# Padded token tiles and eight unread one-column matmuls in a decoder layer on one Trainium2 core

## The chip, the cores and the metric

The kernel runs on one core of one Trainium2 chip. The metric is the device time of one execution in microseconds (us), as a median over several runs. A core has a matmul engine (TensorE, PE in the profile; PEld is its weight load), a vector engine (VectorE, DVE), a scalar engine (ScalarE, ACT), GpSimd (POOL) and SyncE (SP), which issues most DMAs. They run side by side and wait for each other by semaphores. A matmul takes a stationary operand of 128 x 128 (the weights) and streams a moving operand of N columns past it; its result goes to one of eight banks of PSUM, each 512 fp32 columns wide.

## The reference

One step of a hybrid decoder layer is computed for 1024 prompt tokens and 64 sample tokens with shared weights. The part that matters here is the feed-forward block at its end:

```python
def conv_ffn(h, w_up, conv_w, conv_b, w_down, prev):
    z = h @ w_up
    T = z.shape[1]
    zp = jnp.concatenate([prev, z], axis=1)
    c = conv_b + sum(zp[:, j:j + T] * conv_w[j] for j in range(CONV_W))
    a, b = jnp.split(c, 2, axis=-1)
    return (jax.nn.gelu(a) * b) @ w_down, zp[:, T:]
...
    x = x + merged @ w_out
    f, nconv = conv_ffn(rmsnorm(x, norm_ffn), w_up, conv_w, conv_b, w_down, conv_prev)
    return x + f, nk, nv, nconv, vn
```

`w_up` has 1024 rows and 5632 columns, `w_down` 2816 rows and 1024 columns. Ahead of this block stand the input projection, windowed attention, a chunked gate and two output projections; a final RMSNorm stands behind it.

## The kernel before

All products are fp32 in three matmuls: each operand is split into a high and a low part (`th`, `tl` for tokens, `wh`, `wl` for weights), and high x high, low x high and high x low are added in one bank. The splits run on ScalarE (L40, a cast) and VectorE (L41, a subtraction).

The large projections go by a scheme of Strassen's kind: a 2 x 2 block product is made of seven half-size products. The class `Chain` does this for one group of tokens. Group 0 has two halves of 288 columns, group 1 two halves of 256. A token tile holds, for one of four blocks of 128 rows, the seven operands side by side, so `T0` tiles are 7 x 288 and `T1` tiles 7 x 256 columns of 4 bytes. `T0` lies at the right end of the on-chip memory, eight tiles one behind the other, made in `t0_split` (L1562): for each row block the high tile and then the low one. `product(j, w)` (L291) issues the j-th product: 12 matmuls on L301 (four row blocks, three of high and low each) into one bank, and then a copy or an addition that reads the bank.

The up projection (L1699 to L1777) runs over 22 column blocks f. The first three (`FEW`, L1700) run group 0 alone, 7 x 12 matmuls of 288 columns each. Then a loop over `order` (L1756, counter `at`) runs both groups on the 19 others, and group 1 alone on blocks 0, 1 and 2, which stand at `at` 6, 13 and 21. Which group goes first alternates from product to product (L1770), so that two products of 256 columns and two of 288 follow each other in turn: 24 matmuls of one width, 24 of the other. Between the blocks `finish` does convolution, gate and the token operands of the down projection, which go to memory.

The down projection (L1921 to L1958) has 77 units, eleven (`NU`) for each of seven products; `at` counts the products here, `lo` the unit within one. A unit loads and splits a token tile (a ring of tiles of 576 columns) and one half weight tile, and issues 24 matmuls on L1804: four column blocks of 288 columns and four of 256, three matmuls each. Near the end `fin_rms` (L1832) and `fin_rb` (L1848) put small fp32 matmuls of the final norm between units; each of these instructions stands in the trace as two matmuls, called passes below. They use a bank of their own (`psl`).

The order on each engine is that of the code, as the tile scheduler lays it out. Token tiles of the up projection are written once before it; weights come by a ring four deep.

Of the kernel before, what the change touches and what calls it, by code (L numbers as in the profile page):

```python
# [6 lines left out]
F32 = mybir.dt.float32  # L7
F32R = mybir.dt.float32r
# [7 lines left out]
P = 128  # L16
# [18 lines left out]
def layer(tc, a):  # L35
    nc = tc.nc
    V, S, G, PE = nc.vector, nc.scalar, nc.gpsimd, nc.tensor
# [9 lines left out]
    with ExitStack() as top:  # L47
# [26 lines left out]
        ones = cst.tile([P, P], F32, name="c_ones")  # L74
        V.memset(ones, 1.0)
        ident = cst.tile([P, P], F32, name="c_ident")
# [184 lines left out]
        def combine(t4, b11, b12, b21, b22):  # L261
# [3 lines left out]
            V.scalar_tensor_tensor(t4[:, 1], t4[:, 2], -1.0, b11, ALU.mult, ALU.subtract)  # L265
            V.scalar_tensor_tensor(t4[:, 3], t4[:, 1], -1.0, b21, ALU.mult, ALU.subtract)

        def wt(i):
            return a["wt"][i].rearrange("p (k c) -> p k c", c=P)

        class Chain:

# [15 lines left out]
                for to, lo, hi in self.places(e, half):  # L288
                    op(to, pick(x, to, lo, hi), pick(y, to, lo, hi))  # L289

            def product(self, j, w):  # L291
                name = "adadaca"[j]
                first = name not in self.bank
                if first:
                    self.bank[name] = self.ps.tile([P, 512], F32, name="st")[:, :self.n2]
                ps = self.bank[name]
                wh, wl = w
                for kk in range(4):
                    th, tl = (x[:, (0, 1, 2, 6, 3, 5, 4)[j]] for x in self.tx[kk])
                    for i, (u, v) in enumerate(((wh, th), (wh, tl), (wl, th))):  # L300
                        PE.matmul(ps, u[:, kk, :], v, start=first and kk + i == 0,  # L301
                                  stop=kk == 3 and i == 2, skip_group_check=True)
                kept = self.kept
                if j == 0:
                    self.keep("1", ps)
                elif j == 1:
                    self.keep("5", ps)
                elif j == 2:
                    self.keep("u", ps)
                elif j == 3:  # L310
                    self.put(0, 1, V.tensor_add, kept["u"], ps)
                elif j == 4:
                    self.keep("n", ps, -1.0)
                    self.put(1, 1, G.tensor_sub, kept["n"], kept["5"])
                elif j == 5:
                    self.put(0, 0, V.tensor_add, kept["1"], ps)
                else:
                    for to, lo, hi in self.places(1, 0):
                        S.activation(to, pick(ps, to, lo, hi), AF.Copy, scale=-1.0)
# [39 lines left out]
        with ExitStack() as ph1:  # L359
# [1198 lines left out]
            def t0_split(kk):  # L1558

                def go():  # L1560
                    x0, x1, t4 = hx.pop(kk)
                    tx[0][kk] = th, tl = tuple(t0p.tile([P, 7, 288], F32R, name=f"t{y}0{kk}") for y in "hl")  # L1562
                    split(th[:, 0], tl[:, 0], x0[:, 0:288])
                    split(th[:, 5:7], tl[:, 5:7], x1.rearrange("p (h c) -> p h c", h=2))
                    split(th[:, 1:5], tl[:, 1:5], t4)
                return go
# [189 lines left out]
        for at, f in enumerate(order):  # L1756
            if at == NFF - 1:
                t0o.close()
                dn_pools()
                zp.update(z=right(tops, "z2"), za=1)  # L1760
            za, zb = z_pair()
            if f < FEW:
                for e, z in enumerate((za, zb)):
                    nc.sync.dma_start(z[:, 0:594], zd[f][e])
            else:
                put_state(f, (za, zb))
            chains = [up_chain(g, za, zb) for g in ((1,) if f < FEW else (0, 1))]
            for j in range(7):
                w = W.get(3, 1)
                for ch in chains[::1 - 2 * ((7 * at + j) % 2)]:  # L1770
                    ch.product(j, w)
                if f < FEW and j == 3:
                    put_state(f, (za, zb))
            if at < NFF - 2:
                finish(f, za, zb)
            else:
                later.append(lambda f=f, za=za, zb=zb: finish(f, za, zb))  # L1777
        pse.close()

        with ExitStack() as ph3:  # L1780
# [115 lines left out]
            def units(n, count):  # L1896
                out = []
                for x in range(n, n + count):
                    t_upto(x + 5, x + 3)
                    w = W.get(2, 3)  # L1900
                    out.append((w, ts["made"][x]))
                return out
# [18 lines left out]
            for at, j in enumerate(DN_ORDER):  # L1921
# [4 lines left out]
                for lo, hi in blocks:  # L1926
# [10 lines left out]
                    for go in hooks.get((at, lo), ()):  # L1937
                        go()
                    got = units(n0 + lo, hi - lo)
                    for mp in range(2) if hi - lo == 2 else (0,):  # L1940
                        for e in range(2):
                            for x in range(lo, hi):
                                for m in range(2 * mp, 2 * mp + 2) if hi - lo == 2 else range(4):
                                    mm_dn(m, e, x, got[x - lo], new)
                        if hi == NU:
                            for m in (2 * mp, 2 * mp + 1):
                                for e in range(2):
                                    take(j, m, e)
# [134 lines left out]
```

## Time and profile before

| | us |
|---|---|
| median of three runs (lowest, highest) | 1504.83 (1504.61, 1505.7) |
| profiled execution, its own time | 1506.5 |
| its span, first to last instruction | 1504.6 |
| PE busy | 1492.3 |
| DVE, ACT, POOL busy | 1163.4, 832.7, 282.5 |
| L301, share of the chain that ended last | 52% |
| L1804, share of the chain that ended last | 15% |

The profile shows one execution on the hardware. Busy times are sums over an engine's instructions; matmuls overlap, so PE at 99% does not say how close it is to its peak. The clock row gives the granted clock of PE in tenths of full speed, slice by slice. The chain is followed back from the last instruction. In the timeline the first column is the start of an instruction and the second its duration; the difference of two starts is what passes from one matmul to the next.

### The profile page before, as it was taken

How to read it: one execution, taken by the hardware profiler on the slowest of the kernel's cores; microseconds unless marked ns; L12 is line 12 of the kernel's file. 1: busy time of each engine (PE TensorE's matmuls, PEld its weight loads, DVE VectorE, ACT ScalarE, POOL GpSimd, SP SyncE). 2: the span in 40 equal slices, each digit the busy share in tenths (PEclk: the TensorE clock that was granted, in tenths of full speed). 3: DMA queues.
4: the chain of work that ended last, by engine and by line, in shares of the span. 5: the costliest groups of instructions: out<-in, count | busy, mean ns of one | idle time of the engine just before them, and what ended most of it. 6: DMA issues, size and time to landing. Idle time of an engine off the chain costs nothing.

```text
span 1504.6 us, 31437 instructions
## 1 busy us (share of the span) xinstructions
PE 1492.3 (99%) x12169; PEld 1479.7 (98%) x12169; DVE 1163.4 (77%) x1954; ACT 832.7 (55%) x1798; POOL 282.5 (19%) x438
## 2 busy tenths in 40 slices
PE   9999999999999999999999999999999999999998
PEld 8999999999998999999999999999999999999998
DVE  6887779557545986988678888898898888785676
ACT  7656674554554775864444654654555556453463
POOL 2001003100030332430222222232142122000003
PEclk9999999999999999999999999999999999999999
DMA  8552468557659757859977423332332217973454
GB/s 282 182 189 104 165 216 270 176 177 249 216 209 326 236 177 237 246 190 315 337 242 271 142 102 121 119 123 95 116 131 95 109 64 243 362 235 98 121 185 134
DMA packets 136932, 286.10 MB, mean 190 GB/s; under 512 B 15312, under 2 KB 43856, under 8 KB 136784
## 3 DMA queue, kind: packets, MB, share of 16 engines
q1 hardware_dynamic: 131952, 279.57, 55.1%
q10 hardware_dynamic: 4832, 4.54, 0.9%
q8 instruction: 95, 1.56, 0.4%
q14 instruction: 53, 0.43, 0.1%
HBM read 195.56 MB, written 90.46 MB: 190 GB/s over the span
## 4 chain that ended last, share of the span: by engine, by line
PE 94%; DVE 3%; ACT 1%; issue 1%; DMA 0%; SPq 0%; DVEq 0%; ACTq 0%
PE st L301 52%; PE mm L241 15%; PE dn L1804 15%; PE st L538 6%; PE sc L1295 1%; PE po L1356 1%; PE mx L904 1%; PE pt L1328 1%; ACT s L1318 1%; DVE nm L1311 0%; DVE s L1321 0%; DVE s L1305 0%; DMA wh<-xt 0%; PE st L603 0%; DVE of L1367 0%
## 5 line engine op out<-in xcount | busy, mean ns | idle before, releaser
L301 PE MATMUL st<-th,wh 128*128 128x256 f32 (+1 forms) x2128 | 611.4, 287 | 0.3 <-ACT k L282 0.2
L301 PE MATMUL st<-tl,wh 128*128 128x256 f32 (+1 forms) x2128 | 609.7, 287 | 0.0
L301 PE MATMUL st<-th,wl 128*128 128x256 f32 (+1 forms) x2128 | 609.3, 286 | 0.0
L301 PEld LDWEIGHTS st<-th,wh 128*128 128x128 f32 x2128 | 400.6, 188 | 1.3 <-ACT k L282 0.9
L301 PEld LDWEIGHTS st<-th,wl 128*128 128x128 f32 x2128 | 400.9, 188 | 0.0
L301 PEld LDWEIGHTS st<-tl,wh 128*128 128x128 f32 x2128 | 400.4, 188 | 0.0
L40 ACT CAST wh<-wraw 128x512 fp32r<-128x512 f32 (+1 forms) x244 | 144.1, 611 | 85.3 <-PE st L301 33.6
L41 DVE TENSOR_TENSOR wl<-wraw,wh 128x512 fp32r<-128x512 f32 (+1 forms) x244 | 166.1, 696 | 27.3 <-ACT wh L40 25.4
L1804 PE MATMUL dn<-th,wh 128*128 128x288 f32 (+1 forms) x616 | 177.6, 288 | 0.0
L1804 PE MATMUL dn<-tl,wh 128*128 128x288 f32 (+1 forms) x616 | 177.1, 287 | 0.0
L1804 PE MATMUL dn<-th,wl 128*128 128x288 f32 (+1 forms) x616 | 177.0, 287 | 0.0
L40 ACT CAST wh<-ws 128x512 fp32r<-128x512 f32 x160 | 98.0, 622 | 96.5 <-PE st L301 78.3
L41 DVE TENSOR_TENSOR wl<-ws,wh 128x512 fp32r<-128x512 f32 x160 | 109.0, 694 | 50.4 <-ACT wh L40 48.7
L1804 PEld LDWEIGHTS dn<-th,wh 128*128 128x128 f32 x616 | 116.9, 190 | 0.0
L1804 PEld LDWEIGHTS dn<-th,wl 128*128 128x128 f32 x616 | 115.8, 188 | 0.0
L1804 PEld LDWEIGHTS dn<-tl,wh 128*128 128x128 f32 x616 | 115.8, 188 | 0.0
L289 POOL TENSOR_TENSOR z<-ku,k 128x256 f32<-128x256 f32 (+1 forms) x32 | 30.1, 943 | 317.2 <-ACT ku L284 242.4
L40 ACT CAST th<-traw 128x544 fp32r<-128x544 f32 (+1 forms) x85 | 54.1, 643 | 55.6 <-PE dn L1804 42.9
L41 DVE TENSOR_TENSOR tl<-traw,th 128x544 fp32r<-128x544 f32 (+1 forms) x85 | 61.0, 725 | 23.3 <-ACT th L40 23.1
L241 PE MATMUL mm<-s,wh 128*128 128x256 f32 (+1 forms) x384 | 76.5, 295 | 0.0
L282 ACT COPY k<-st 128x256 f32<-128x256 f32 (+1 forms) x152 | 56.0, 381 | 35.2 <-PE st L301 34.2
L241 PE MATMUL mm<-oh,wh 128*128 128x256 f32 (+1 forms) x256 | 73.6, 288 | 0.0
(311 smaller groups left out, 3187.2 us busy)
## 6 DMA issues: line engine op xcount, KB each, us to landing
wraw<-wt SPq DMA_DIRECT2D x133, 512.0 KB
traw<-td SPq DMA_DIRECT2D x77, 272.0 KB
td<-za SPq DMA_DIRECT2D x22, 544.0 KB
wraw<-wt SPq DMA_DIRECT2D x35, 256.0 KB
upd<-hl SPq DMA_DIRECT2D x14, 512.0 KB
td<-t SPq DMA_DIRECT2D x11, 544.0 KB
qd<-q SPq DMA_DIRECT2D x8, 576.0 KB
q<-qd SPq DMA_DIRECT2D x8, 576.0 KB
```

Of the source, the lines that this page charges most:

```text
L40: S.copy(hi, src)
L41: V.tensor_sub(lo, src, hi.bitcast(F32))
L241: PE.matmul(ps[:, lo:lo + c1 - c0], u[:, k, :], v[:, c0:c1], start=(clear and k == 0 and i == 0), stop=(k == nk - 1 and i == 2), skip_grou ...
L282: S.copy(t, src)
L289: op(to, pick(x, to, lo, hi), pick(y, to, lo, hi))
L301: PE.matmul(ps, u[:, kk, :], v, start=first and kk + i == 0, stop=kk == 3 and i == 2, skip_group_check=True)
L538: PE.matmul(ps, u, v[:, k, :], start=k + i == 0, stop=k == KD - 1 and i == 2)
L904: PE.matmul(ps[:, P * i:P * i + P], vn[:, i], late["wst"][:, c, :], start=True, stop=True)
L1295: PE.matmul(ps[:, h, o0:256], q, kst[kv][:, e, k0:cur + P], start=e == 0, stop=e == 1)
L1318: S.activation(s[:, h], s[:, h], AF.Exp, bias=nm[:, h:h + 1], accum_out=dn[:, h:h + 1])
L1328: PE.transpose(pt[:, h * P:h * P + P], s[:, h, 0:P], ident)
L1804: PE.matmul(place(m, e), u[:, m, :], v[:, lo:hi], start=new and i + k == 0 and (e == 0 or m != 1), stop=i == NU - 1 and k == 2, skip_group ...
```

## The change

Two things are added. First, the `T0` tiles are allocated 2048 columns long and used as 7 x 288 = 2016 (`sevens`), so that their starts are 8192 bytes apart in place of 8064. Second, `unread` issues two fp32 matmuls of one column, the identity by a column of ones, into the last two columns of a bank, where nobody reads them. It is called at four places: ahead of a product of group 0 in the bank that this product is about to use, where `at` is 0, 7 and 14 (product 1, 0 and 1), and in the down projection at unit 2 of its second product, in the bank of `fin_rms`.

```diff
+        def sevens(t):
+            return t[:, 0:7 * 288].rearrange("p (j c) -> p j c", c=288)
...
+        def unread(ps):
+            for i in range(2):
+                PE.matmul(ps[:, 510 + i:511 + i], ident, ones[:, 0:1], start=True, stop=True, skip_group_check=True)
...
-            def product(self, j, w):
+            def product(self, j, w, spare=False):
                 name = "adadaca"[j]
                 first = name not in self.bank
                 if first:
-                    self.bank[name] = self.ps.tile([P, 512], F32, name="st")[:, :self.n2]
+                    full = self.ps.tile([P, 512], F32, name="st")
+                    self.bank[name] = full[:, :self.n2]
+                    if spare:
+                        unread(full)
...
-                    tx[0][kk] = th, tl = tuple(t0p.tile([P, 7, 288], F32R, name=f"t{y}0{kk}") for y in "hl")
+                    tx[0][kk] = th, tl = tuple(sevens(t0p.tile([P, 2048], F32R, name=f"t{y}0{kk}")) for y in "hl")
...
-                    ch.product(j, w)
+                    ch.product(j, w, at % 7 == 0 and j < 2 and (7 * at + j) % 2 == 1 and ch.g == 0)
...
+                    if (at, lo) == (1, 2):
+                        unread(psl.tile([P, 512], F32, name="fs", bufs=1))
```

On PE, at the first of the four places, the last matmuls of a 256-column product stand next to the first of a 288-column one before the change (out <- moving tile, weights; then the shape of the result; 10785, 10868, 11314 and 11336 are buffer numbers):

```order
L301 MATMUL st<-th_11336,wh 128x256
L301 MATMUL st<-tl_11337,wh 128x256
L301 MATMUL st<-th_11336,wl 128x256
L301 MATMUL st<-th_10785,wh 128x288
L301 MATMUL st<-tl_10786,wh 128x288
```

With the change (L301 is L311 there):

```order
L311 MATMUL st<-th_11336,wh 128x256
L311 MATMUL st<-tl_11337,wh 128x256
L311 MATMUL st<-th_11336,wl 128x256
L276 MATMUL st<-c_ones,c_ident 128x1 x2
L311 MATMUL st<-th_10785,wh 128x288
L311 MATMUL st<-tl_10786,wh 128x288
```

Two instructions stand between the two products, and nothing else on PE has moved there.

On PE in the down projection, between unit 12 and unit 13, before the change:

```order
L1804 MATMUL dn_17059<-th,wh 128x256
L1804 MATMUL dn_17059<-tl,wh 128x256
L1804 MATMUL dn_17059<-th,wl 128x256
L1804 MATMUL dn<-th,wh 128x288
L1804 MATMUL dn<-tl,wh 128x288
```

With the change (L1804 is L1814 there, `fs` the bank of `fin_rms`):

```order
L1814 MATMUL dn_17065<-th,wh 128x256
L1814 MATMUL dn_17065<-tl,wh 128x256
L1814 MATMUL dn_17065<-th,wl 128x256
L276 MATMUL fs<-c_ones,c_ident 128x1 x2
L1814 MATMUL dn<-th,wh 128x288
L1814 MATMUL dn<-tl,wh 128x288
```

Again two instructions come between two blocks of different width.

On ACT in the up projection, in the column block at 7, before the change (`ku` and `k` are copies out of banks, `wh` a weight split):

```order
L1737 ACTIVATE za<-c 128x64
L282 COPY k_13449<-st 128x288
L282 COPY k_13464<-st 128x256
L40 CAST wh<-ws 128x512
L40 CAST wh<-wraw 128x512
L282 COPY ku<-st 128x256
L40 CAST wh<-wraw 128x512
L282 COPY ku<-st 128x288
```

With the change (L282 is L289, L1737 is L1747 there):

```order
L1747 ACTIVATE za<-c 128x64
L289 COPY k_13453<-st 128x288
L289 COPY k_13468<-st 128x256
L40 CAST wh<-ws 128x512
L40 CAST wh<-wraw 128x512 x2
L289 COPY ku<-st 128x256
L289 COPY ku<-st 128x288
```

One cast has moved ahead of one copy; VectorE has the matching swap, and both have one more in the down projection.

## Rows read from the trace of the kernel before

**Rows 1.** The page's engine table (busy us, share, instructions) and clock row.

```profile
PE 1492.3 (99%) x12169; PEld 1479.7 (98%) x12169; DVE 1163.4 (77%) x1954; ACT 832.7 (55%) x1798; POOL 282.5 (19%) x438
...
PEclk9999999999999999999999999999999999999999
```

**Rows 2.** The chain of work that ended last, by line.

```profile
PE st L301 52%; PE mm L241 15%; PE dn L1804 15%; PE st L538 6%; PE sc L1295 1%; PE po L1356 1%; PE mx L904 1%; PE pt L1328 1%; ACT s L1318 1%; DVE nm L1311 0%; DVE s L1321 0%; DVE s L1305 0%; DMA wh<-xt 0%; PE st L603 0%; DVE of L1367 0%
```

**Rows 3.** Waits of PE from 800 to 1490 us: total us, times, longest.

```profile
PE st L301 <- ACT k L282: 0.2, 1, 0.2
```

**Rows 4.** Windows: length, busy us by engine (instructions), clock, DMA share, GB/s.

```profile
807.00:838.50 31.50, 31.50 (x239) 31.50 (x239) 31.27 (x64) 18.67 (x42) 6.03 (x7) 1.00 0.59 210
...
1302.00:1448.00 146.00, 146.00 (x1173) 146.00 (x1172) 101.20 (x178) 66.36 (x120) 0.00 (x0) 1.00 0.57 181
```

**Rows 5.** Timeline of PE, up projection: start us, us, instruction; block starts.

```profile
838.78 0.28 PE L301 MATMUL st<-th,wh 128*128 128x256 f32 x1
...
839.25 0.28 PE L301 MATMUL st<-tl,wh 128*128 128x256 f32 x1
...
841.52 0.29 PE L301 MATMUL st<-th,wh 128*128 128x288 f32 x1
...
844.69 0.28 PE L301 MATMUL st<-th,wh 128*128 128x256 f32 x1
...
957.16 0.28 PE L301 MATMUL st<-th,wh 128*128 128x256 f32 x1
```

**Rows 6.** Timeline of PE, down projection, one unit: starts of its blocks.

```profile
1304.92 0.28 PE L1804 MATMUL dn<-th,wh 128*128 128x256 f32 x1
...
1306.33 0.30 PE L1804 MATMUL dn<-th,wh 128*128 128x288 f32 x1
...
1307.91 0.28 PE L1804 MATMUL dn<-th,wh 128*128 128x256 f32 x1
```

**Rows 7.** Timeline of PE, down projection, around four passes of fin_rms.

```profile
1458.11 0.28 PE L1804 MATMUL dn<-th,wh 128*128 128x256 f32 x1
...
1459.53 0.50 PE L1841 MATMUL fs<-c_ones,acc 128*128 128x1 f32 x4
1459.89 0.38 PE L1804 MATMUL dn<-th,wh 128*128 128x288 f32 x1
...
1461.56 0.28 PE L1804 MATMUL dn<-th,wh 128*128 128x256 f32 x1
...
1462.92 0.30 PE L1804 MATMUL dn<-th,wh 128*128 128x288 f32 x1
```

**Rows 8.** Timeline of PE, down projection, two later units: block starts.

```profile
1475.87 0.29 PE L1804 MATMUL dn<-th,wh 128*128 128x288 f32 x1
...
1477.45 0.28 PE L1804 MATMUL dn<-th,wh 128*128 128x256 f32 x1
...
1478.81 0.29 PE L1804 MATMUL dn<-th,wh 128*128 128x288 f32 x1
...
1481.76 0.29 PE L1804 MATMUL dn<-th,wh 128*128 128x288 f32 x1
```

**Rows 9.** Timeline of PE, down projection, behind six passes of fin_rms.

```profile
1450.01 0.59 PE L1841 MATMUL fs<-c_ones,acc 128*96 128x1 f32 x6
...
1452.12 0.28 PE L1804 MATMUL dn<-th,wh 128*128 128x256 f32 x1
...
1453.54 0.30 PE L1804 MATMUL dn<-th,wh 128*128 128x288 f32 x1
```

**Rows 10.** Timeline of PE, branch products: block starts.

```profile
702.31 0.28 PE L241 MATMUL mm<-oh,wh 128*128 128x256 f32 x1
...
703.67 0.30 PE L241 MATMUL mm<-mh,wh 128*128 128x320 f32 x1
...
707.19 0.28 PE L241 MATMUL mm<-mh,wh 128*128 128x256 f32 x1
...
710.02 0.31 PE L241 MATMUL mm<-mh,wh 128*128 128x320 f32 x1
```

## The prediction

> **What bounds the kernel now.** I read the page's engine table and its clock row first. PE, the engine of the matmuls, is busy 1492.3 us of a span of 1504.6 us, and the clock row stands at 9 in every slice [rows 1]; the granted clock is 1.00 in the stretches used below [rows 4], so this is the 2.4 GHz level throughout. The chain of work that ended last says the same: the up and gate products of L301 hold 52% of the span and the down projection of L1804 15% [rows 2]. Last come the waits: from 800 us to 1490 us PE waited 0.2 us in all [rows 3]. Nothing is late for PE in the two stages that the change touches. What can move is only the number of matmuls and the distance from the start of one to the start of the next, which I call the spacing. The mean duration in a table of groups does not give it, since matmuls overlap; it is read from the start column of the timeline, over blocks of equal matmuls.
>
> **What the spacings are.** In the down projection a unit is 12 matmuls of 288 columns and 12 of 256. The 256-column block takes 1306.33 - 1304.92 = 1.41 us, 117.5 ns each, and the whole unit 2.99 us [rows 6]. That holds until 1459.53 us. There two one-column matmuls of fin_rms stand (four passes in the trace, since an fp32 matmul is issued twice), and after them the 256-column block takes 1462.92 - 1461.56 = 1.36 us, 113.3 ns each, where the block just ahead took 1.42 us [rows 7]. It stays so: two units from 1475.87 to 1481.76 us take 5.89 us, 2.945 us each, with 1.36 us for 256 columns and 1.58 us for 288 [rows 8]. So the same instructions run in one of two steady rhythms, **slow** (117.5 ns at 256 columns) and **fast** (113.3 ns), and something short in the stream can switch them. Not each insertion does: after six passes with 96-column weights at 1450.01 us a unit still takes 1453.54 - 1452.12 = 1.42 us for its 256-column block [rows 9].
>
> In the up projection blocks of 24 alternate. A 256-column block takes 841.52 - 838.78 = 2.74 us, 114.2 ns each; its first four start 0.47 us apart, 117.5 ns each, so it enters slow and falls into the fast rhythm by itself. A 288-column block takes 844.69 - 841.52 = 3.17 us. Twenty such pairs, 838.78 to 957.16 us, take 118.38 us, 5.919 us a pair [rows 5]; so over the long run a 288-column block is 3.18 us, 132.4 ns each. The same 48 matmuls take 2 x 2.945 = 5.89 us in the fast rhythm of the down projection and 5.98 us in the slow one [rows 6, 8].
>
> **The change part by part.** The sum is made against the profiled span of 1504.6 us; that execution's own time was 1506.5 us and the median of the three runs is 1504.83 us, and I take the differences off the median.
>
> *The unread matmuls.* Four places, two matmuls each, four passes. Their price is read where the kernel has the same thing already: from 1459.53 us to the first wide matmul at 1459.89 us is 0.36 us, and the wide block behind it takes 1461.56 - 1459.89 = 1.67 us in place of 1.58 us, 0.09 us more [rows 7, 8]. That is 0.45 us a place, **+1.8 us** in all. PE is the bound, so nothing hides it. Their operands, the identity and the ones, are written once at the start, and the bank written is one that the next product waits for anyway (in the down projection the small bank of fin_rms, idle until then).
>
> *The switch in the down projection.* The place is unit 13 of 77, and fin_rms stands at unit 66, so 53 units can be fast that were slow: 53 x (2.99 - 2.945) = **-2.4 us**. The bounds are 0, if these passes act like the six at 1450 us, and -2.4 us. I take the full gain, since the four passes at 1459.53 us are the nearest row: as many passes, as many weight columns, and also between a 256-column block and a 288-column block.
>
> *The padding.* A T0 tile has 7 x 288 x 4 = 8064 bytes, 31.5 times 256, so the high and the low part of each token block lie 128 bytes apart within 256. With 8192 bytes they lie alike, as the 256-column set's (7168 bytes, 28 x 256) and the down projection's ring (2304 bytes, 9 x 256) do. The padding costs no instruction, and the trace of before has no such T0, so its effect is bounded by rows. The up projection has 19 column blocks of 7 products on both groups, 19 x 7 x 24 matmuls, 66.5 pairs of 48. If these settle in the fast rhythm, as the down stage shows for evenly laid tiles, a pair goes from 5.919 to 5.89 us: 66.5 x 0.029 = **-1.9 us**. If they settle in the slow rhythm it goes to 5.98 us: +4.1 us. I take the fast end, because each of the three long stretches gets one of the unread pairs at its start, and the only such insertion ahead of a 288-column block (1459.53 us) left the fast rhythm behind it.
>
> *The first blocks.* Column blocks 0 to 2 run group 0 alone, 252 matmuls of 288 columns. The window from 807.0 to 838.5 us holds 239 in 31.50 us, two of them in flight at an edge: 132.9 ns [rows 4]. At 1.58 us for 12 [rows 8] it is 131.7 ns: 252 x 1.2 ns = 0.3 us. I take **-0.2 us**.
>
> *What the scheduler moved.* On ScalarE and on VectorE two neighbours change places in the up projection (a cast or subtraction for the weights goes ahead of a step on a bank) and once more in the down projection. PE waited 0.2 us in 690 us [rows 3], with eight banks to rotate through; I cost this at nothing, and at 0.2 us if that cover were gone. SyncE and GpSimd keep their order.
>
> Sum: 1.8 - 2.4 - 1.9 - 0.2 = -2.7 us. Forecast: 1504.8 - 2.7 = **1502.1 us**.
>
> **The rivals.**
>
> *The up projection locks slow.* Evenly laid tiles keep a rhythm, and they keep the wrong one as well. For it: in the branch products a 12-matmul stretch of 256 columns took 703.67 - 702.31 = 1.36 us, then 24 of 320 columns followed, and the next 24 of 256 took 710.02 - 707.19 = 2.83 us, 117.9 ns each [rows 10]: a wide block turned fast into slow, in evenly laid tiles, and no block of 24 there fell back. Today's up projection always falls back within four matmuls, and the padding may take that away. Price: 1.8 - 2.4 + 4.1 - 0.2 = +3.3 us, 1508.1 us. It decides from 30 of the 66.5 pairs on: 30 x 0.061 - 36.5 x 0.029 = +0.8 us, which with 1.8 - 2.4 - 0.2 makes no change. If one of the three stretches locks, the time is near 1504.1 us; with two, 1506.1 us.
>
> *The padding changes nothing.* The blocks still enter slow and fall back. Then 1.8 - 2.4 = -0.6 us, 1504.2 us. Against it stands that a wide block of evenly laid tiles has no such fall-back behind it [rows 6, 10]. In the Trainium skill, "SBUF — State Buffer", Specifications, cachelines are 16 bytes; by that a shift of 128 bytes would leave the reads as they are, and this case results. No run here shows yet whether it is so.
>
> *The down projection is not switched.* As at 1450.01 us [rows 9]. Then 1.8 - 1.9 - 0.2 = -0.3 us, 1504.5 us.
>
> *The wide matmuls come down too.* At 2.4 GHz 256 columns are 106.7 ns, and the fast rhythm is 113.3 ns, 6.6 ns above; 288 columns with the same addition would be 126.6 ns, not 132.4 ns. On the 1848 wide matmuls of the up projection (66.5 x 24 + 252) that is -10.7 us, and with 24 x 66.5 x 0.9 ns = -1.4 us at 256 columns, -2.4 us and +1.8 us the time is 1492.1 us. Against it: in the down projection's even tiles 12 wide ones take 1.58 us in both rhythms [rows 6, 8]. The Trainium skill, "TensorE: Matmul & The Clock Gate", Back-to-back issue gap, gives N/2.4 + 2.5 ns for a warm isolated gap, 122.5 ns at 288 columns; by that an estimate of the gain at 288 columns would be 18 us. The rows contradict it at 256 columns already, with 113.3 ns where it has 109.2 ns.
>
> **How the numbers follow.** Forecast 0.50; padding without effect 0.12; down not switched 0.08; some of the up stretches slow 0.10; all of them slow 0.13; wide ones faster 0.07. The range takes in all but the last two: the low end is the forecast less 1.5 us (the wide blocks a little nearer the down stage's, 66.5 x 24 x 0.7 ns = 1.1 us, and 0.4 us of rounding in the starts), 1500.6 us; the high end 1507.2 us is above two slow stretches, 1506.1 us. What a measurement here tells from no change is 0.2%, 3.0 us: below 1501.8 us and above 1507.8 us. The forecast lies 0.3 us inside the lower line; with its spread some four in ten of it are beyond, 0.20, and the wide-matmul case adds 0.07. Of the all-slow case, 0.3 us beyond the upper line, six in ten are slower, 0.08, and two slow stretches with an unseen wait add 0.04. So faster 0.27, same 0.61, slower 0.12.
>
> **What will show it.** Each step has its mark in the timeline of the changed kernel: 0.45 us more at each of the four places; a 256-column block of the down projection at 1.36 us from unit 13 on; a pair of up blocks at 5.89 us, with the first four of 24 at 113 ns. Up blocks of 24 at 2.83 us would mean the slow lock; 2.74 us with four slow ones ahead, that the padding did nothing; 288-column blocks below 3.1 us, that the wide ones moved. The forecast is wrong if PE shows new waits of more than 0.5 us, or if the one-column matmuls cost more than 0.6 us a place.

## The result, and the profile after

The changed kernel took 1508.61 us in the median of 9 runs (1507.39 to 1513.15), the kernel before beside it 1504.61 us (9 runs): a ratio of 1.0028, 95% interval 1.0018 to 1.0038. It is slower by about 4 us, against a forecast of 1502.1 us with a range up to 1507.2 us. The profiled execution took 1513.15 us with a span of 1511.1 us, so it lies 4.5 us above the median, and the one of before (1506.5 us) 1.9 us above its own; what of this belongs to the kernel and what to one execution had to be told apart first. Two runs that are far longer than all others, one of e5 at 5188.77 us and one of the kernel before beside it at 1533.05 us, are left out of every ratio below.

PE is still the bound. The page's engine table and clock row of the changed kernel answer to [rows 1]:

```profile
PE 1496.9 (99%) x12185; PEld 1483.3 (98%) x12185; DVE 1163.4 (77%) x1954; ACT 832.1 (55%) x1798; POOL 278.3 (18%) x438
...
PEclk9999999999999999999999999999999999999999
```

There are 16 more passes and the clock row is unchanged. The waits of PE from 800 to 1490 us (total us, times, longest) are the same 0.2 us as in [rows 3]:

```profile
PE st L311 <- ACT k L289: 0.2, 1, 0.2
```

So PE's own list has no new wait in the two stages, and the time must be in the spacing of matmuls (one wait of the weight load, which this list leaves out, comes below). First the length of the up projection, from the first row of its first product to the first row of the down projection, in the timeline of PE (start us, us, instruction). Before:

```profile
800.78 0.29 PE L301 MATMUL st<-th,wh 128*128 128x288 f32 x1
...
1261.43 0.30 PE L1804 MATMUL dn<-th,wh 128*128 128x288 f32 x1
```

and after, with the first unread pair and five block starts behind it, which answer to [rows 5]:

```profile
803.55 0.29 PE L311 MATMUL st<-th,wh 128*128 128x288 f32 x1
...
844.35 0.50 PE L276 MATMUL st<-c_ones,c_ident 128*128 128x1 f32 x4
844.71 0.38 PE L311 MATMUL st<-th,wh 128*128 128x288 f32 x1
...
853.88 0.28 PE L311 MATMUL st<-th,wh 128*128 128x256 f32 x1
...
856.70 0.30 PE L311 MATMUL st<-th,wh 128*128 128x288 f32 x1
...
859.88 0.28 PE L311 MATMUL st<-th,wh 128*128 128x256 f32 x1
...
862.61 0.29 PE L311 MATMUL st<-th,wh 128*128 128x288 f32 x1
...
865.78 0.28 PE L311 MATMUL st<-th,wh 128*128 128x256 f32 x1
...
1267.29 0.29 PE L1814 MATMUL dn<-th,wh 128*128 128x288 f32 x1
```

The up projection went from 1261.43 - 800.78 = 460.65 us to 1267.29 - 803.55 = 463.74 us, 3.1 us longer. Of two 256-column blocks of 24 that follow each other, one takes 856.70 - 853.88 = 2.82 us (117.5 ns each, slow from its first matmul to its last) and the next 862.61 - 859.88 = 2.73 us (fast throughout), where before each takes 2.74 us, four matmuls at 117.5 ns and the rest in the fast rhythm. Over the stage 27 of 65 such blocks keep the slow rhythm, in a pattern that comes back every seven blocks; the mean of a block is 2.766 us, 2.743 us before. The up projection also begins 2.8 us later (803.55 against 800.78 us). This start moves between executions of one kernel too, as the table below shows, and whether the change has a part in it is not settled.

The down projection, in the same view, around the unread pair and around fin_rms's four passes (the place of [rows 7]):

```profile
1298.34 0.28 PE L1814 MATMUL dn<-th,wh 128*128 128x256 f32 x1
...
1299.70 0.29 PE L1814 MATMUL dn<-th,wh 128*128 128x288 f32 x1
...
1301.62 0.28 PE L1814 MATMUL dn<-th,wh 128*128 128x256 f32 x1
...
1303.03 0.30 PE L1814 MATMUL dn<-th,wh 128*128 128x288 f32 x1
...
1306.03 0.50 PE L276 MATMUL fs<-c_ones,c_ident 128*128 128x1 f32 x4
1306.39 0.38 PE L1814 MATMUL dn<-th,wh 128*128 128x288 f32 x1
...
1308.05 0.28 PE L1814 MATMUL dn<-th,wh 128*128 128x256 f32 x1
...
1309.46 0.30 PE L1814 MATMUL dn<-th,wh 128*128 128x288 f32 x1
...
1465.65 0.50 PE L1851 MATMUL fs<-c_ones,acc 128*128 128x1 f32 x4
...
1467.68 0.28 PE L1814 MATMUL dn<-th,wh 128*128 128x256 f32 x1
...
1469.05 0.29 PE L1814 MATMUL dn<-th,wh 128*128 128x288 f32 x1
```

Here stands what the forecast did not think of. At 1298.34 us, ahead of any unread matmul of this stage, the block takes 1.36 us: the stage began in the fast rhythm. The 288-column block from 1299.70 us takes 1.92 us in place of 1.58 us, and the next 256-column block 1.41 us: it has turned slow. The unread pair at 1306.03 us leaves it slow (1309.46 - 1308.05 = 1.41 us), and only fin_rms's passes at 1465.65 us turn it fast (1.37 us). The chain of waits has VectorE in this block (start us, us, what), and the timeline of the weight load (PEld) has what waited for it:

```profile
1299.22 0.68 DVE wl L41
1299.91 0.37 DVE x L1824
...
1300.33 0.19 PEld L1814 LDWEIGHTS dn<-th,wh 128*128 128x128 f32 x1 [0.30 <-DVE x L1824]
```

The addition that frees the product bank (L1824) stood behind a subtraction for the weights. The weight load waited 0.30 us for it, and the next matmul came some 0.2 us late in this execution.

### The profile page after: what moved, and what is told of

Read it like the earlier page. It is cut to its first block, busy times and chain, and to the rows that moved or that the text cites. A ratio compares the mean times of both kernels' runs of the same rounds, so it can differ in the third digit from the quotient of the medians.

```text
span 1511.1 us, 31469 instructions
## 1 busy us (share of the span) xinstructions
PE 1496.9 (99%) x12185; PEld 1483.3 (98%) x12185; DVE 1163.4 (77%) x1954; ACT 832.1 (55%) x1798; POOL 278.3 (18%) x438
## 4 chain that ended last, share of the span: by engine, by line
PE 88%; DVE 7%; ACT 2%; DMA 1%; issue 1%; SPq 0%; POOL 0%; ACTq 0%; DVEq 0%
PE st L311 52%; PE mm L241 15%; PE dn L1814 15%; PE st L548 2%; PE sc L1305 1%; PE po L1366 1%; PE mx L914 1%; DVE tl L41 1%; DMA gvd<-gv 1%; DVE s L1331 1%; DVE nm L1321 1%; PE pt L1338 1%; ACT s L1328 1%; DVE s L1315 0%; DVE wl L41 0%
## 5 line engine op out<-in xcount | busy, mean ns | idle before, releaser
L311 PE MATMUL st<-th,wh 128*128 128x256 f32 (+1 forms) x2128 | 611.4, 287 | 1.7 <-ACT k L289 1.6
L311 PE MATMUL st<-tl,wh 128*128 128x256 f32 (+1 forms) x2128 | 609.5, 286 | 0.0
L311 PE MATMUL st<-th,wl 128*128 128x256 f32 (+1 forms) x2128 | 608.6, 286 | 0.0
L311 PEld LDWEIGHTS st<-th,wh 128*128 128x128 f32 x2128 | 400.7, 188 | 2.8 <-ACT k L289 2.3
L311 PEld LDWEIGHTS st<-th,wl 128*128 128x128 f32 x2128 | 400.0, 188 | 0.0
L311 PEld LDWEIGHTS st<-tl,wh 128*128 128x128 f32 x2128 | 399.7, 188 | 0.0
L1814 PE MATMUL dn<-th,wh 128*128 128x288 f32 (+1 forms) x616 | 177.4, 288 | 0.1
L1814 PE MATMUL dn<-tl,wh 128*128 128x288 f32 (+1 forms) x616 | 176.7, 287 | 0.0
L1814 PE MATMUL dn<-th,wl 128*128 128x288 f32 (+1 forms) x616 | 176.4, 286 | 0.0
L1814 PEld LDWEIGHTS dn<-th,wh 128*128 128x128 f32 x616 | 116.5, 189 | 0.3 <-DVE x L1824 0.3
L1814 PEld LDWEIGHTS dn<-th,wl 128*128 128x128 f32 x616 | 115.7, 188 | 0.0
L1814 PEld LDWEIGHTS dn<-tl,wh 128*128 128x128 f32 x616 | 115.6, 188 | 0.0
L289 ACT COPY k<-st 128x256 f32<-128x256 f32 (+1 forms) x152 | 56.1, 381 | 34.9 <-PE st L311 34.0
L241 PE MATMUL mm<-oh,wl 128*128 128x256 f32 (+1 forms) x256 | 73.5, 287 | 0.0
```

The lines of the kernel that those rows point to most:

```text
L241: PE.matmul(ps[:, lo:lo + c1 - c0], u[:, k, :], v[:, c0:c1], start=(clear and k == 0 and i == 0), stop=(k == nk - 1 and i == 2), skip_grou ...
L289: S.copy(t, src)
L311: PE.matmul(ps, u[:, kk, :], v, start=first and kk + i == 0, stop=kk == 3 and i == 2, skip_group_check=True)
L1814: PE.matmul(place(m, e), u[:, m, :], v[:, lo:hi], start=new and i + k == 0 and (e == 0 or m != 1), stop=i == NU - 1 and k == 2, skip_group ...
```

## The experiments

All kernels compute the same result as the kernel before. The times of four kernels of a group (e1 to e4, e5 to e8, e9 to e12, e13 to e16) stand beside runs of the kernel before on the same chip, and each group ran on another chip. The ratios are the recorded estimates with their 95% intervals; they are not the quotients of two medians (for e1, 1507.96 us beside 1504.48 us would be 1.0023).

**Table of the profiled executions**, worked out from the start column of PE's timeline. Up begins: start of its first matmul. Up: from there to the first matmul of the down projection. 256: mean of its 65 blocks of 24, and how many took over 2.8 us. Last six: spacing of the last six matmuls of the up projection. Down 256: the first 256-column block of the down projection, 12 matmuls. Down: from its first matmul to the start of its last. All times in us, the spacing in ns.

| kernel | up begins | up | 256 | slow | last six | down 256 | down |
|---|---|---|---|---|---|---|---|
| before | 800.78 | 460.65 | 2.743 | 1 | 117.7 | 1.41 | 233.8 |
| e5, before again | 802.73 | 460.62 | 2.743 | 1 | 113.3 | 1.36 | 230.8 |
| e2, unread only | 801.06 | 461.75 | 2.744 | 1 | 113.3 | 1.36 | 231.3 |
| e4, unread in down only | 802.09 | 460.47 | 2.743 | 1 | 113.3 | 1.36 | 231.2 |
| e6, 2080 columns | 800.96 | 460.45 | 2.743 | 1 | 113.3 | 1.36 | 231.0 |
| e1, padding only | 802.68 | 462.77 | 2.774 | 32 | 113.3 | 1.36 | 230.8 |
| e7, 2112 columns | 802.13 | 463.48 | 2.778 | 34 | 113.3 | 1.36 | 230.8 |
| e8, high tiles only | 804.29 | 463.57 | 2.786 | 37 | 113.3 | 1.36 | 231.2 |
| e9, 2032 columns | 803.13 | 460.95 | 2.734 | 1 | 113.3 | 1.36 | 231.4 |
| e10, 2024 columns | 801.48 | 459.64 | 2.723 | 0 | 113.5 | 1.36 | 230.7 |
| e16, the same again | 803.82 | 459.64 | 2.726 | 1 | 113.3 | 1.36 | 230.7 |
| e12, 2040 columns | 803.86 | 459.19 | 2.740 | 0 | 117.7 | 1.41 | 233.8 |
| e3, padding and unread in up | 802.49 | 463.59 | 2.768 | 28 | 113.3 | 1.36 | 230.7 |
| e15, the change with 2024 | 804.61 | 460.92 | 2.723 | 0 | 113.3 | 1.36 | 231.3 |
| after | 803.55 | 463.74 | 2.766 | 27 | 113.3 | 1.36 | 234.0 |
| e11, after again | 804.70 | 463.77 | 2.766 | 27 | 117.7 | 1.41 | 234.3 |
| e13, after, third | 804.31 | 463.53 | 2.766 | 27 | 113.3 | 1.36 | 231.3 |
| e14, after, fourth | 803.26 | 463.55 | 2.768 | 28 | 113.3 | 1.36 | 231.2 |

### The parts of the change apart (e1 to e4)

The theory: the padding makes the up projection lose its fall into the fast rhythm. The rival: the unread matmuls set the slow rhythm and the padding is innocent.

**e1_pad_only** leaves out all unread matmuls:

```diff
-                ch.product(j, w, at % 7 == 0 and j < 2 and (7 * at + j) % 2 == 1 and ch.g == 0)
+                ch.product(j, w)
```

> Padded T0 tiles alone, no unread matmuls. Theory A (the padding makes the up projection lose its fall-back): some blocks of 24 matmuls of 256 columns stay at 118 ns all through, as in the changed kernel, where 115.25 ns stood on the mean against 114.31 ns before; 1560 such matmuls x 0.94 ns = +1.5 us, and 288-column blocks +0.3 ns x 1560 = +0.5 us: 1506.6 us. Theory B (the unread matmuls set the slow rhythm and the padding is innocent): all up blocks of 24 within 114.5 ns on the mean and the time within 0.5 us of before.

Measured: 1507.96 us, ratio 1.0015 (1.0006 to 1.0024). Two neighbouring blocks of 256 columns in its timeline:

```profile
846.65 0.28 PE L311 MATMUL st<-th,wh 128*128 128x256 f32 x1
...
849.48 0.30 PE L311 MATMUL st<-th,wh 128*128 128x288 f32 x1
...
852.67 0.28 PE L311 MATMUL st<-th,wh 128*128 128x256 f32 x1
...
855.39 0.29 PE L311 MATMUL st<-th,wh 128*128 128x288 f32 x1
```

2.83 us and 2.72 us: the mixture of whole slow and whole fast blocks is there with no unread matmul in the kernel. The up projection is 2.1 us longer than before. The padding does it, and the rival is out. The unread pairs shift the pattern a little: 32 slow blocks here, 27 and 28 with the pairs (after, e3).

**e2_unread_only** undoes the padding:

```diff
-tuple(sevens(t0p.tile([P, 2048], F32R, name=f"t{y}0{kk}")) for y in "hl")
+tuple(t0p.tile([P, 7, 288], F32R, name=f"t{y}0{kk}") for y in "hl")
```

> The eight unread matmuls alone, T0 tiles as before. Theory A: the up projection keeps 114.3 ns a 256-column matmul, each place costs 0.45 us, the down projection is switched or not by chance: +1.8 us, or -0.6 us if it is switched from unit 13 on. Theory B: up blocks at 118 ns in a good part of the blocks behind the three places, +3 us or more.

Measured: 1507.6 us, ratio 1.0017 (1.0008 to 1.0025), runs from 1505.49 to 1510.31 us. The blocks are those of before (2.744 us), and the up projection is 1.1 us longer for three pairs. The stages account for 1.1 + 0.45 = 1.6 us; the interval holds that.

**e3_pad_and_up** leaves out only the pair of the down projection:

```diff
-                    if (at, lo) == (1, 2):
-                        unread(psl.tile([P, 512], F32, name="fs", bufs=1))
```

> Padding and the three unread pairs of the up projection, nothing in the down projection. Theory A: as the padding alone plus 3 x 0.45 = 1.35 us, with the same pattern of slow and fast up blocks (3 of 7 slow). Theory B: +3.4 us against before, of which all but 0.2 us would come from the three pairs. Against the changed kernel it lacks one pair, 0.45 us.

Measured: 1508.07 us, ratio 1.0023 (1.0014 to 1.0032); up 463.59 us, as in the whole change.

**e4_down_only** keeps only that pair (no padding, no pair in the up projection).

> Only the unread pair of the down projection. If the pair switches slow to fast as the four passes of fin_rms do: 256-column blocks at 1.36 us from unit 13 on, -2.4 + 0.45 = -2.0 us, 1502.6 us. If it does not: 1.41 us all through, +0.45 us, 1505.1 us. In the changed kernel's profile the pair stood in a slow stretch and left it slow, so I expect the second.

Measured: 1504.91 us, ratio 1.0003 (0.9994 to 1.0012). The rows at the pair:

```profile
1299.51 0.28 PE L1814 MATMUL dn<-th,wh 128*128 128x256 f32 x1
...
1300.87 0.50 PE L276 MATMUL fs<-c_ones,c_ident 128*128 128x1 f32 x4
1301.23 0.38 PE L1814 MATMUL dn<-th,wh 128*128 128x288 f32 x1
...
1302.90 0.28 PE L1814 MATMUL dn<-th,wh 128*128 128x256 f32 x1
```

The four passes take 0.36 us and the wide block behind them 1.67 us, the 0.45 us of the prediction. But the block ahead of them already takes 1.36 us: in all of e1 to e4 the down projection is fast from its start, at 230.7 to 231.3 us against the 233.8 us of before's profile. There was nothing to switch.

### Where the tiles lie (e6 to e8)

If the even start of high and low tiles is the cause, another uneven padding must be harmless and another even one must not.

**e6_pad_2080** (8320 bytes, 32.5 times 256: high and low tile 128 bytes apart within 256, as before):

```diff
-tuple(sevens(t0p.tile([P, 2048], F32R, name=f"t{y}0{kk}")) for y in "hl")
+tuple(sevens(t0p.tile([P, 2080], F32R, name=f"t{y}0{kk}")) for y in "hl")
```

> Padding alone, but to 2080 columns (8320 bytes, an odd number of 128) instead of 2048: high and low tiles then start 128 bytes apart within 256, as they do in the kernel before with 8064 bytes, while the room taken is larger than in the change. Theory A (the slow blocks come of high and low tiles starting at the same place within 256 bytes): up projection as before, 256-column blocks mean 114.3, all but the first four or five at 113.4, 288-column blocks 132.4, the projection 460.5 to 461 us, time 1504.5. Rival S (any gap between the tiles, or their moved places, does it): blocks between 113 and 118 in a pattern again, mean 115.3, projection 462.5 to 463.5 us, time 1506.5 to 1507.5.

Measured: ratio 0.9997 (0.9988 to 1.0006), up 460.45 us. Its blocks:

```profile
850.78 0.28 PE L311 MATMUL st<-th,wh 128*128 128x256 f32 x1
...
853.52 0.29 PE L311 MATMUL st<-th,wh 128*128 128x288 f32 x1
...
856.69 0.28 PE L311 MATMUL st<-th,wh 128*128 128x256 f32 x1
```

2.74 and 3.17 us, those of [rows 5]: more room between the tiles costs nothing.

**e7_pad_2112** (8448 bytes, 33 times 256; 2112 in place of 2080 in the same line).

> Padding alone, to 2112 columns (8448 bytes, 33 times 256): high and low tiles start at the same place within 256 bytes, but at other distances and places than in the change. Theory A: as with the change's padding, 256-column blocks in a pattern of 113 and 118, mean 115.3, projection 462.5 to 463.5 us, time 1506.5 to 1507.5. Rival S would give the same; a rival P (it is the power of two in the distance of 8192 bytes that counts) gives the up projection of before, 460.5 to 461 us, 1504.5.

Measured: ratio 1.0011 (1.0002 to 1.002), up 463.48 us, 34 slow blocks. The even start hurts at another distance too, so the power of two is not what counts.

**e8_pad_high** pads the high tiles alone, so that the two tiles of one k (one of the four row blocks) start alike and each next k 128 bytes on:

```diff
+tuple(sevens(t0p.tile([P, 2048 if y == "h" else 2016], F32R, name=f"t{y}0{kk}")) for y in "hl")
```

> Only the high tiles padded to 2048 columns, the low ones left at 2016: high and low tile of one k start at the same place within 256 bytes, and each next k 128 bytes on. If theory A's cause lies between the high and the low tile of one k (the three products of one weight pair), the up projection is as with the change, mean 115.3 and 462.5 to 463.5 us; if it lies between one k and the next, it is as before, 114.3 and 460.5 to 461 us; a pattern of its own would show that both count.

Measured: ratio 1.0013 (1.0004 to 1.0022), up 463.57 us, 37 slow blocks. One of them:

```profile
848.22 0.28 PE L311 MATMUL st<-th,wh 128*128 128x256 f32 x1
...
851.05 0.30 PE L311 MATMUL st<-th,wh 128*128 128x288 f32 x1
```

2.83 us. The cause lies between the high and the low tile of one k, which the 288-column matmuls read in turn. With e6 and e7 this settles it for the distances tried: 0 bytes modulo 256 between the two hurts, 128 bytes does not. The effect is not where the padding is, though. The blocks that turn slow are those of 256 columns; they read the `T1` tiles, 7168 bytes long (28 times 256) in every kernel here. These lie evenly in the kernel before as well, where 64 of 65 blocks fall back. The offset of the `T0` tiles thus acts on the blocks that come behind those which read them. What in the hardware makes it so, no run shows.

### Other offsets (e9, e10, e12, e16)

**e9_pad_2032**, **e10_pad_2024** and **e12_pad_2040** put the two tiles 64, 96 and 32 bytes apart, by that number alone. The step from one row block to the next changes with it (128, 64 and 64 bytes within 256, 0 in the kernel before), so a gain among these three may come from either.

> Padding alone, to 2032 columns (8128 bytes): the high and the low tile of one k start 64 bytes apart within 256, halfway between the kernel before (128 apart) and the change (0 apart). Theory A in its graded form (the spacing depends on how far apart they start): 256-column blocks between 114.3 and 115.7 in the mean, the projection between 460.5 and 463 us. In its form of yes and no (only an even start hurts): 114.3 and 460.5 to 461 us, 1504.5 to 1506.5 us as the kernel before beside it. If 128 is not the best distance, blocks nearer to 113.4 throughout: down to 1.4 us off the projection.

> Padding alone, to 2024 columns (8096 bytes): high and low tile of one k start 96 bytes apart within 256. Graded form: nearer to the kernel before than the 64-byte one, 114.3 to 115; yes and no: 114.3, projection 460.5 to 461 us.

> Padding alone, to 2040 columns (8160 bytes): high and low tile of one k start 32 bytes apart within 256. Graded form: nearer to the change than the 64-byte one, 115 to 116 and 462 to 463.5 us; yes and no: 114.3 and 460.5 to 461 us.

Measured: at 64 bytes the up projection takes 460.95 us, at 96 bytes 459.64 us, at 32 bytes 459.19 us, at most 0.3 us longer than before and up to 1.5 us shorter. So the loss is not graded by the distance: of the five offsets only the even start has it. Neither form had foretold the gains at 96 and 32 bytes; the expectation of e9 had allowed for a better distance than 128. The gains are of two kinds: at 96 bytes the 256-column blocks are fast from their first matmul (2.723 us), at 32 bytes the 288-column blocks are shorter (3.161 us, 3.177 before). The blocks of e10:

```profile
845.40 0.28 PE L311 MATMUL st<-th,wh 128*128 128x256 f32 x1
...
848.12 0.29 PE L311 MATMUL st<-th,wh 128*128 128x288 f32 x1
...
851.30 0.28 PE L311 MATMUL st<-th,wh 128*128 128x256 f32 x1
```

The times are 1.0016 (1.0007 to 1.0024) for e9, 0.9988 (0.9979 to 0.9997) for e10 and 1.0004 (0.9995 to 1.0014) for e12. The 1.0016 of e9 is not in its two stages (460.95 and 231.4 us) and stays open; a ratio 0.1 to 0.2% from 1 is therefore no proof of a cause by itself, and the stage lengths carry the argument. The up projection of e12 is the shortest of all and its time is no shorter; in its profile the down projection is slow (233.8 us), and whether it was in the other runs is not known. **e16_pad_2024_again** ran e10 a second time:

> Padding to 2024 columns alone, in another execution: up projection 459.5 to 459.8 us, 256-column blocks 113.5 (they are set by where the tiles lie, so every time), ratio to the kernel before 0.999 to 1.000, since 0.8 us of 1505 is all that the blocks can give. Chance alone in the first run of it would put the ratio at 1.000 or above and the blocks back to 114.3.

Measured: up 459.64 us as expected, and a ratio of 0.9985 (0.9976 to 0.9994), a little below what was expected. Padding to 2024 columns without unread matmuls is faster than the kernel before by 1.0 us in the up projection, twice and on two chips. That is 0.07% of the time; the two ratios are 0.12 and 0.15% below 1, and both intervals hold 0.07%.

### Whose the rhythm of the down projection is (e5, e11, e13, e14, e15)

**e5_before_again** is the kernel before, unchanged.

> The kernel before, unchanged, in another execution. Theory C (the down projection's rhythm is a chance state of one execution: the profiled execution before the change, 1.9 us above the median, was in its slow rhythm for 66 units, and the usual execution is in the fast one from the start, as in the four runs that were profiled so far): the down projection takes 230.5 to 231.5 us instead of 233.8, every block of it near 113.5 ns a column group, and the profiled execution comes out 2 to 3 us shorter than the one of 1506.5 us, at 1503.5 to 1504.9. Rival D (before is slow in it every time, and the four kernels were fast because each of them had moved something): 233.8 us again, slow until fin_rms's four passes, and about 1506.5 us. Up projection the same for both: 256-column blocks 114.3, 288-column blocks 132.4.

Measured: 0.9995 (0.9986 to 1.0004). The rows of its first unit in the down projection:

```profile
1263.35 0.29 PE L1804 MATMUL dn<-th,wh 128*128 128x288 f32 x1
...
1264.93 0.28 PE L1804 MATMUL dn<-th,wh 128*128 128x256 f32 x1
...
1266.29 0.29 PE L1804 MATMUL dn<-th,wh 128*128 128x288 f32 x1
```

1.36 us, fast from the start: the same program as in [rows 6], where it is 1.41 us. The profiled time, 1505.89 us, was 1 us above what was expected, though; the up projection began 1.95 us later here.

**e11_after_again**, **e13_after_third** and **e14_after_fourth** are the changed kernel, unchanged.

> The changed kernel in another execution. Theory C (the rhythm in which the down projection starts, and the 2.8 us that its profiled execution lost ahead of 800 us, belong to that execution): the down projection fast from its start, 231 to 231.5 us with the unread pair in it, not 234.0; up projection 463 to 464 us as before, since the padding acts every time; profiled execution 1508 to 1510 us, not 1513; ratio to the kernel before 1.002 to 1.003. Rival D (the change itself makes the down projection slow, by where its instructions lie): 234 us again and a profiled execution of 1511 us or more.

This was a miss: 1514.36 us in the profiled execution, ratio 1.0039 (1.0024 to 1.0054), and the down projection slow from its start:

```profile
1267.76 0.28 PE L311 MATMUL st<-th,wh 128*128 128x256 f32 x1
...
1268.47 0.30 PE L1814 MATMUL dn<-th,wh 128*128 128x288 f32 x1
...
1270.05 0.28 PE L1814 MATMUL dn<-th,wh 128*128 128x256 f32 x1
...
1271.46 0.30 PE L1814 MATMUL dn<-th,wh 128*128 128x288 f32 x1
...
1307.39 0.50 PE L276 MATMUL fs<-c_ones,c_ident 128*128 128x1 f32 x4
...
1309.40 0.28 PE L1814 MATMUL dn<-th,wh 128*128 128x256 f32 x1
...
1310.82 0.30 PE L1814 MATMUL dn<-th,wh 128*128 128x288 f32 x1
```

The first row is the sixth matmul from the end of the up projection: 0.71 us for six. Then 1.41 us ahead of the unread pair and 1.42 us behind it: a second time the pair did not switch it. With most of this stage at 1.41 us a block in two profiles of the changed kernel out of two, the theory that the change itself makes the stage slow could not be put aside.

> The changed kernel in a third execution. If the down projection only inherits the rhythm in which the last twelve matmuls of the up projection run, after the wait on ScalarE in that last block (theory I), its rhythm is a draw of one execution: fast here with some chance (11 of 14 executions of all kernels so far started it fast), then 231 to 231.5 us and about 1510 us; where the last twelve are at 118, 234 us and 1513 us. Rival D (the change's instructions make it slow) has it slow even after a last block at 113.

> The same once more: by theory I the first block of the down projection goes as the last twelve matmuls of the up projection do, 113 or 118. By rival D it is slow in this execution too, whatever ended the up projection.

Measured, one run each: 1510.68 and 1510.42 us, and both fast from the start. The rows of e13, again from the sixth matmul before the stage's end (0.68 us for six):

```profile
1267.16 0.28 PE L311 MATMUL st<-th,wh 128*128 128x256 f32 x1
...
1267.84 0.29 PE L1814 MATMUL dn<-th,wh 128*128 128x288 f32 x1
...
1269.43 0.28 PE L1814 MATMUL dn<-th,wh 128*128 128x256 f32 x1
...
1270.79 0.29 PE L1814 MATMUL dn<-th,wh 128*128 128x288 f32 x1
```

The table's columns "last six" and "down 256" say what decides it. In 18 of 18 executions the down projection begins in the rhythm in which the up projection ends: 1.41 us behind 117.7 ns (before, e11, e12), 1.36 us behind 113.3 to 113.5 ns (the other fifteen). The same kernel does either. Where two executions of it part can be read too. Counted from the first matmul of the up projection, the starts in before and e5 lie within 10 ns of each other up to its last product. The first matmul of that product comes late in both, 190 and 196 ns behind the one ahead of it; from the product's sixth matmul on e5 is at 113 ns, and before stays at 118 ns. That the end of the one stage causes the start of the other is what these rows suggest; no run forced it. Nor is the chip ruled out as what decides: no two executions of one kernel that differ are known to share a chip, and e9 and e10 (fast) ran on one chip with e11 and e12 (slow), but as other kernels.

**e15_after_2024** is the whole change with 2024 columns.

> The whole change, but padded to 2024 columns (high and low tile of one k 96 bytes apart) instead of 2048. If only the even start hurts, the 256-column blocks are at 113.5 all through, with the three unread pairs the up projection is 459.65 + 3 x 0.45 = 461.0 us (463.7 with the change's padding), and the time is 2.5 to 3 us below the changed kernel's: ratio to the kernel before 1.0005 to 1.001 instead of 1.0028. If padding and unread matmuls together do something that neither does alone, it stays above 462.5 us.

Measured: ratio 1.0000 (0.9991 to 1.001), up 460.92 us with no slow block. The unread matmuls add their own price to e10's 459.64 us and nothing else, and the even start was the padding's loss in the whole change too.

## Why the prediction was wrong, step by step

**Unread matmuls: right.** 0.36 us of passes (844.35 to 844.71 us) and a wide block of 1.66 us (1306.39 to 1308.05 us). Four pairs were to cost 1.8 us; e2 has 1.1 us for three in the up projection (1.35 us forecast). For the one in the down projection the rows of e4 give 0.36 + 0.09 = 0.45 us; its ratio of 1.0003 (0.9994 to 1.0012) is too coarse to show that.

**The switch in the down projection: wrong, -2.4 us forecast, 0 measured.** It failed twice. The slow rhythm ahead of unit 66 was taken for a property of the kernel, and it is not in every execution: e5 has the same stage at 230.8 us. The 1.7 us between the profiled execution and the median stood in the prediction, and the differences were taken off the median as if it had the same slow stage; they should have been read as a sign that this execution might have something the median did not have. And where the stage was slow (after, e11), the pair did not switch it, though it has as many passes and weight columns as fin_rms's, and stands between the same kinds of blocks. fin_rms's own four passes did turn the stage fast in all four executions that met them slow, so "I take the full gain, since the four passes at 1459.53 us are the nearest row" rested on something real; what sets the two apart, no run shows. A single occurrence, with a counter-example in [rows 9], had been taken at full value: those six passes, too, stand ahead of a 288-column block (the one between them and the block at 1452.12 us), though the prediction calls the one at 1459.53 us the only such insertion there. That it did not switch was the rival with 0.08.

**The padding: wrong in sign, -1.9 us forecast, +2.1 us measured (e1).** The step that failed is "I take the fast end". That the fall-back would go came true: 256-column blocks now keep for all 24 matmuls the rhythm in which they start. The ground given for it, that evenly laid tiles keep a rhythm, does not hold as it stands, since the `T1` tiles that these blocks read were evenly laid before too, and 64 of 65 blocks fell back; it is the layout of the `T0` tiles read in between that counts (e8). That an unread pair at the head of a stretch would then set every later block fast was wrong: across the 288-column blocks in between the rhythm changes again and again, in a pattern of seven blocks, and some three in seven come out slow. This is the first rival, but its price was off. It had every pair at 5.98 us; the mean pair of after is 2.766 + 3.185 = 5.951 us, against 5.920 us (2.743 + 3.177): 65 x 0.031 = 2.0 us, which with the unread passes counted apart (3 x 0.36 = 1.1 us) makes the 3.1 us of the stage.

By the page "SBUF — State Buffer" of the Trainium skill, Specifications (TRN2), cachelines are 16 bytes long. From that the prediction had drawn a rival in which a shift of 128 bytes, eight whole lines, changes nothing. The runs contradict that reading: 0 bytes apart and 128 bytes apart differ by 2.1 us in this stage (e1, before), and 128 bytes apart at another distance does not (e6).

**The first blocks: 0 in place of -0.2 us.** The 240 matmuls of 288 columns behind the first token blocks take 31.97 us after and 31.92 us before.

**The scheduler's swaps: right at nothing** in the two stages [rows 3]. Ahead of 800 us the waits of PE differ from one execution to the next, also of the same kernel; the up projection begins between 800.78 and 804.70 us in the 18 executions. The four executions of the changed kernel begin it at 803.26 to 804.70 us, the two of the kernel before at 800.78 and 802.73 us, the two with 2024 columns alone (e10, e16) at 801.48 and 803.82 us; whether the change has a part in that is not settled.

**The sum as it should have been:** 1.1 us for the unread pairs of the up projection, 2.1 us for the padding, 0.45 us for the pair in the down projection and no switch, +3.6 us, a ratio of 1.0024. The measured interval (1.0018 to 1.0038) holds it, and that of e11 (1.0024 to 1.0054) does at its edge. The first rival's 1508.1 us is near the measured 1508.61 us for a wrong reason: its up projection was 2 us too dear, and its down projection 2.4 us too cheap.

**The chances.** The cases were set up as exclusive, each with one step going wrong. Two steps went wrong at once, the padding and the switch, and together they lie above the range; their independent chances should have been multiplied into cases of their own.

## What to carry to other kernels

When a profiled execution is longer than the median by more than the change can give, its stages are first compared with those of a second execution of the same kernel, before a gain is built on a state seen in one of them. Where three matmuls read a high and a low tile in turn, the offset of the two tiles is a parameter worth trying: here 0 bytes modulo 256 cost 2.1 us of 460.6 us, and 96 bytes gained 1.0 us. The blocks to look at are then not only those that read these tiles: here the 256-column blocks changed, and no run changed how their own tiles lie to each other. A short insertion into a tight stream is costed at its own price alone: one kind of insertion switched the rhythm in four executions of four, another of equal length in none of two, and nothing seen here tells beforehand which kind a new one is.

## What the runs showed of the hardware that was not expected

- Matmuls with equal shapes and equal weight loads run at 113.3 or 117.7 ns for 256 columns at the same granted clock, and which of them depends on the offset between the high and the low moving tile of the 288-column blocks in between, and on what ran just ahead. Offsets of 0, 32, 64, 96 and 128 bytes modulo 256 between those two tiles gave mean 256-column blocks of 2.774, 2.740, 2.734, 2.723 and 2.743 us.
- The rhythm goes on from one stage into the next: in 18 of 18 executions the down projection began as the up projection had ended, which is worth some 3 us of 1505 us (233.8 and 230.8 us for the kernel before).
- One addition on VectorE that the weight load waited for (1299.91 us) stood ahead of a turn from fast to slow that lasted 55 units, and the four passes of fin_rms turned the stage fast each time they met it slow (before, after, e11, e12), while the four passes of an unread pair did not (after, e11).
